# A decoder layer on one core: three seven-product pairs in each double gate block, and other paces for the background multiply-adds

## The chip, the cores and the metric

The kernel runs on one core of one Trainium2 chip. The metric is the device time of one execution in microseconds (us), as the median of repeated runs. The profile shows one execution, taken by the hardware profiler.

## The reference, cut to what matters

One layer of a hybrid decoder for 256 tokens of width 2048, all in float32. `h` is the normalised input, modulated by vectors that come out of `silu(c) @ w_ada`; that product has six segments of 2048 columns, and the later ones (for the second norm and the gates) aren't needed until late in the layer.

```python
mod = jax.nn.silu(c) @ w_ada[l] + b_ada[l]
shift1, scale1, gate1, shift2, scale2, gate2 = jnp.split(mod[:, None, :], N_MOD, axis=-1)
h = rms_norm(x, norm1_gain[l]) * (1 + scale1) + shift1
x = x + gate1 * mixing_sublayer(h, w_in[l], ...)
h = rms_norm(x, norm2_gain[l]) * (1 + scale2) + shift2
x = x + gate2 * swiglu(h, w_ffn_in[l], w_ffn_out[l])
...
proj = h @ w_in              # in mixing_sublayer; the last 3 * 2048 columns are gate_cols
...
g = jax.nn.sigmoid(gate_cols.reshape(b, t, N_BRANCH, d))
y = (g[:, :, 0] * (o_sb @ w_br_sb) + g[:, :, 1] * (o_dil @ w_br_dil) + g[:, :, 2] * (o_gla @ w_br_gla))
return y @ w_out
```

The change is in how `gate_cols` is computed and in when the products with `w_ada` are done.

## The kernel before, in words

The two row tiles of 128 tokens stay on chip, and every weight matrix is streamed from HBM once, in raw blocks of 512 KB (two chunks of 128 rows by 512 columns) by the queue of the SP engine. TensorE takes its operands in a rounded format, so each float32 operand is kept as a high and a low part: ScalarE casts the raw block to the high part `whi` (L165, L236), VectorE subtracts it from the raw block to get `wlo` (L166, L222), and each product is three matmuls in `mm3`: high by high (L173), with the low part of the weights (L174), with the low part of the activations (L175). Their names in the profile give the result, then the weight and the stationary operand; `H` are the parts of h.

The stages are: the modulation for the first norm; the input projection in four groups of chunks (the last is `LAST`), with the three attention branches behind it; the gate stage; the y stage (`y_block`, branch outputs by gates); the output projection; the second norm; eleven FFN units and their output.

The gate stage is this: three single `gate_block`s for the first 512 columns of each branch, then three `gate_pair`s, each for two column blocks of one branch at once. A `gate_pair` calls `fast_products` over eight chunk pairs in the order of `GATE_PAIRS`. A tuple there is (chunk pair, fast). A plain pair makes 8 block products, 24 matmuls. A fast pair makes them with 7, 21 matmuls, in the way of Strassen and Winograd: it needs sums of the four blocks of h (`sums_of_h`, made once) and of the four weight blocks (`load_pair`, on VectorE, in tiles A0 and A1, which are then split too), and at the end of the block the shared partial results are merged (L313 to L316 and L272). Before, pairs 4 and 5 of each double block are fast.

Raw blocks land in a ring of four `raw` tiles and whatever `more_raws` adds; the high and low parts lie in rings of four `whi` and `wlo`, and whatever `more_rooms` adds: X1 and X2, A9 and A10. Before, the double blocks have 5, 6 and 5 raw tiles (T3 and X2 added) and 6, 5 and 5 rooms. `load` runs up to `LOOK` = 3 pairs ahead of the products.

The later segments of the modulation are a background generator. Each step, a *multiply-add*, loads 512 KB of w_ada (L517, into AR0, AR1, KC or KD) and does one 128x1024 operation on VectorE (`ada_mac`, L421, into T4, T5 and others). `tick` is called in the loops of products, and lets out multiply-adds at `state["rate"]`. A multiply-add is issued after the split that `state["split"]` holds. Before, the generator starts with the last group's first blocks, but at a rate of 0, and gets its first rate, `RATE_IN` = 0.8, some blocks later; in the double gate blocks the rate is `RATE_PAIRS` = 0.42.

A scheduler puts the instructions in order for each engine from the program's order, priorities (`prio`) and the tiles that come free; each engine then runs its list in order.

Of the kernel before, what the change touches and what calls it, by code (L numbers as in the profile page):

```python
# [29 lines left out]
N_DIL = 6  # L30
N_GLA = 4
SEG_SHIFT1, SEG_SCALE1, SEG_GATE1, SEG_SHIFT2, SEG_SCALE2, SEG_GATE2 = range(6)
RATE_IN, RATE_MID, RATE_GATES, RATE_PAIRS, RATE_Y, RATE_LAST = 0.8, 0.6, 0.65, 0.42, 0.5, 0.7

RATES_OP, RATES_FFN, RATE_OUT = (0.85, 0.5, 0.0), (0.75, 0.9, 0.7, 0.6), 0.5
GATE2_CUT = 12
# [13 lines left out]
OUT_B = ((0, 0), (1, 0)) + tuple(x for a, b in zip((8, 9, 10, 11, 12, 13, 6, 7), (2, 3, 4, 5, 14, 15, 16, 17)) for x in ((a, 1), (b, 0)))  # L50
PAIRS = ((0, 0), (1, 0), (5, 1), (2, 0), (6, 1), (7, 1), (3, 0), (4, 0))
PAIRS_4 = ((0, 0), (1, 0), (4, 1), (5, 1), (2, 0), (6, 1), (7, 1), (3, 0))
GATE_PAIRS = ((0, 0), (1, 0), (4, 1), (2, 0), (3, 0), (5, 1), (6, 0), (7, 0))
FOUR = (2, 3, 5, 6, 8)
RANK = 16
ROW_N1, ROW_N2, ROW_SBQ, ROW_SBK, ROW_DILQ, ROW_DILK, ROW_GB, ROW_GG = 16, 32, 48, 49, 50, 51, 52, 56
# [24 lines left out]
def trunk(ctx: ExitStack, tc: tile.TileContext, I, out):  # L81
# [16 lines left out]
    def S(tag, shape, dtype=F32):  # L98
        return slot.tile(shape, dtype, tag=tag, name=nm(tag))
# [27 lines left out]
    def tick(n):  # L127
        state["due"] = state.get("due", 0.0) + n
        while state["due"] >= 1.0:
            state["due"] -= 1.0  # L130
            for work in (bg, after):
                if work and next(work[0], "end") == "end":
                    work.pop(0)
# [67 lines left out]
    def sums_of(sf, h, a, b):  # L201

        (a0, b0), (a1, b1) = ((x[:, a, :], x[:, b, :]) for x in h)
        for dst, x, y, op in (
            (0, a1, b1, ALU.add), (2, a0, a1, ALU.subtract), (1, sf[:, 0], a0, ALU.subtract), (3, b0, sf[:, 1], ALU.subtract)
        ):
            nc.vector.tensor_tensor(sf[:, dst], x, y, op=op)

    def load_pair(src, p, c0, c1, fast, tags):


        def raw_at(c):
            more_raws = state.get("more_raws", ())
            i = state["raws"] = (state.get("raws", -1) + 1) % (4 + len(more_raws))
            raw = S(more_raws[i], [P, 2, NB]) if i < len(more_raws) else wp.tile([P, 2, NB], F32, tag="raw", name=nm("raw"))
            nc.sync.dma_start(raw, src[2 * p * P : (2 * p + 2) * P, c : c + NB].rearrange("(k p) c -> p k c", p=P))
            return raw

        def sub(dst, x, y):
            chain = state.get("chain")  # L220
            with tc.issue_after(chain.ins) if chain is not None else nullcontext():
                done = nc.vector.tensor_tensor(dst, x, y, op=ALU.subtract)  # L222
            if "chain" in state:
                state["chain"] = done
            return done

        def split(src):
            n = src.shape[1]
            more_rooms = state.get("more_rooms", ())
            i = state["tiles"] = (state.get("tiles", -1) + 1) % (4 + len(more_rooms))  # L230
            if i < len(more_rooms):
                hi, lo = (S(tag, [P, 2, NB], F32R) for tag in more_rooms[i])
            else:
                hi = wp.tile([P, 2, NB], F32R, tag="whi", name=nm("whi"), bufs=4)
                lo = wp.tile([P, 2, NB], F32R, tag="wlo", name=nm("wlo"), bufs=4)
            nc.scalar.copy(hi[:, :n, :], src)  # L236
            state["split"] = sub(lo[:, :n, :], src, hi[:, :n, :].bitcast(F32))
            return [(hi[:, i, :], lo[:, i, :]) for i in range(n)]

        with prio():  # L240
            if not fast:
                return [split(raw_at(c0)), split(raw_at(c1))]
            r0, r1 = raw_at(c0), raw_at(c1)
            b11, b21 = split(r0)
            ta, tb = (S(tag, [P, 2, NB]) for tag in tags)
            sub(ta[:, 0], r1[:, 0], r0[:, 0])
            sub(ta[:, 1], r1[:, 1], r1[:, 0])
            (b22,) = split(r1[:, 1:2])
            sub(tb[:, 0], r1[:, 1], ta[:, 0])
            sub(tb[:, 1], r0[:, 1], tb[:, 0])  # L250
            t1, t3 = split(ta)
            t2, t4 = split(tb)
            return b11, b21, b22, t1, t3, t2, t4

    def fast_products(src, c0, c1, order, at, sums, own, other, tags, hooks={}, more=False, look=None):


        ws = []

        def load(n):  # L260
            while len(ws) < min(n, len(order)):
                ws.append(load_pair(src, order[len(ws)][0], c0, c1, order[len(ws)][1], tags))


        soon = AHEAD if hooks or more else 2 * AHEAD
        load(look or (LOOK if hooks else len(order)))
        o = [[own([P, NB]) for _ in range(NT)] for _ in range(2)]
        shared = []
        end = len(order)
        first_fast, last_fast = (f(n for n, (_, fast) in enumerate(order) if fast) for f in (min, max))  # L270
        last_plain = max(n for n in range(last_fast) if not order[n][1])
        add = lambda dst, x: nc.vector.tensor_tensor(dst, dst, x, op=ALU.add)  # L272

        def merge(half):
            with prio(soon):
                add(o[0][half], (first, third)[half])
                add(o[1][half], u[:, 1 - half])

        for n, (p, fast) in enumerate(order):
            tick(2 * state["rate"])  # L280
            if n in hooks:
                hooks[n]()
            load(n + LOOK)
            w = ws[n]
            if n == 1 and later:
                with tc.issue_after(state["mm"].ins), prio():
                    later.pop()()
            for half in range(2):
                if n == last_fast + 2 + half:
                    merge(half)  # L290
            merged = n > last_fast
            if fast:
                if not shared:
                    shared = [other([P, NB]) for _ in range(4)]
                    p1, p5, p7, p6 = shared
                s = sums[p]
                a, b = 2 * p, 2 * p + 1
                lefts = (at(a, 0), at(b, 0), s[3], s[0], s[2], s[1], at(b, 1))
                for dst, (h, l), (wh, wl) in zip((p1, o[0][0], o[1][0], p5, p7, p6, o[0][1]), lefts, w):
                    mm3(dst, h, l, wh, wl, n == first_fast and any(dst is x for x in shared), n == last_fast)  # L300
            else:
                for c in range(2):
                    for t in range(NT):
                        for k in range(2):
                            h, l = at(2 * p + k, t)

                            closed = n == end - 1 and not more or merged or (c, t) == (1, 1) and n == last_plain
                            mm3(o[c][t], h, l, *w[c][k], n == 0 and k == 0, k == 1 and closed, merged)
            if n == last_fast:
                with prio(soon):  # L310
                    u, first, third = S("KC", [P, 2, NB]), S("T6", [P, NB]), scr([P, NB])
                    nc.scalar.copy(first, p1)
                    nc.vector.tensor_tensor(u[:, 0], p6, first, op=ALU.add)  # L313
                    nc.vector.tensor_tensor(u[:, 1], p5, u[:, 0], op=ALU.add)
                    nc.vector.tensor_tensor(third, p7, u[:, 0], op=ALU.add)
                    nc.vector.tensor_tensor(u[:, 0], p5, third, op=ALU.add)  # L316
        for half in range(2):
            if end <= last_fast + 2 + half:
                merge(half)
        return o  # L320
# [822 lines left out]
        yield from last_macs()  # L1143

    bg.append(background())
    for b in range(0, 3):
        proj_block(LAST, b)
    qk_norm(sb_parts)
# [57 lines left out]
                gates[1 + i, br] = g  # L1206

    def sums_of_h():
        j = 2
        full = S("X1", [P, 4, T])  # L1210
        nc.vector.tensor_tensor(full, hT[0][j].bitcast(F32), hT[1][j].bitcast(F32), op=ALU.add)
        sf = S("X2", [P, 4, 2, P])
        sums_of(sf, [full[:, :, t * P : (t + 1) * P] for t in range(NT)], slice(0, 4, 2), slice(1, 4, 2))
        hi, lo = (S(tag, [P, 4, 2, P], F32R) for tag in ("T1", "T2"))
        nc.scalar.copy(hi, sf)
        nc.vector.tensor_tensor(lo, sf, hi.bitcast(F32), op=ALU.subtract)
        return {2 * j + m: [(hi[:, i, m, :], lo[:, i, m, :]) for i in range(4)] for m in range(2)}

    with prio():
        groups = dil_weights()  # L1220
# [91 lines left out]
    h_sums = sums_of_h()  # L1312
    state["rate"] = RATE_PAIRS
    ring["tags"], ring["spare"] = ("AR0", "AR1", "KD"), 1
    gate_pair(0, acc_bank, misc_bank, (("X1", "X2"), ("A9", "A10")), ("T3",))
    gate_pair(1, misc_bank, acc_bank, (("A9", "A10"),), ("X2", "T3"))
    gate_pair(2, acc_bank, misc_bank, (("A9", "A10"),), ("T3",))
    ring["tags"] = ("AR0", "AR1", "KC", "KD")
    ring["spare"] = 2
    state["rate"] = RATE_Y  # L1320
# [340 lines left out]
```

## Time and profile before

| | |
|---|---|
| median of 3 runs | 1577.7 us (1575.83 to 1578.93) |
| the profiled execution | 1579.31 us |
| its span, first to last instruction | 1577.5 us |
| mean granted TensorE clock | 0.999 |
| TensorE matmuls (PE) | 1564.6 us busy, 99% |
| VectorE (DVE) | 1394.3 us busy, 88% |
| ScalarE (ACT) | 876.0 us busy, 56% |
| DMA | 402.26 MB, mean 255 GB/s |

TensorE is busy nearly all the time. Busy shares of the other engines are averages over stages; the gate stage runs from about 492 to 622 us of the span, its double blocks are the part of it that the change edits, and the last group's first blocks lie around 250 us. A row of a timeline is: start in us, duration in us, engine, line, operation, out<-in, shape and count, and in brackets the idle time ahead of it with what ended it.

### The profile page before, as it was taken

What the parts mean: (1) busy time and instruction counts of PE and PEld (TensorE: products, weight loads), DVE (VectorE), ACT (ScalarE), POOL (GpSimd) and SP (SyncE); (2) the same over time, 40 slices, a digit from 0 to 9 for tenths busy, and PEclk for the clock granted to TensorE, in tenths of its full rate; (3) what the DMA queues carried; (4) which work ended last, traced back from release to release, by engine and by line L of the source; (5) the groups of instructions that cost most, each with busy time, mean ns of one, the idle gap of its engine ahead of it and who ended that gap; (6) DMA issues with size and microseconds to landing.
All of it is one profiled execution on the core that took longest, in us unless ns stands there. A gap on an engine that the chain in (4) does not pass through costs nothing.

```text
span 1577.5 us, 20267 instructions
## 1 busy us (share of the span) xinstructions
PE 1564.6 (99%) x7186; PEld 1294.6 (82%) x7186; DVE 1394.3 (88%) x1704; ACT 876.0 (56%) x1215; POOL 12.9 (1%) x24
## 2 busy tenths in 40 slices
PE   8999999999999999999999999999999999999998
PEld 7878888888888788888888888888888888888887
DVE  6889996888889899987977888999999999899896
ACT  5654448875765545344445645556555555455553
POOL 1000000000000000000000000000000000000000
PEclk9999999999999999999999999999999999999999
DMA  9999997677788888989897886565666566876664
GB/s 334 360 326 324 336 304 239 221 238 227 233 294 265 269 267 270 313 261 324 291 336 260 304 294 211 190 213 188 199 199 215 174 200 228 293 227 202 222 211 137
DMA packets 196317, 402.26 MB, mean 255 GB/s; under 512 B 13102, under 2 KB 28116, under 8 KB 196216
## 3 DMA queue, kind: packets, MB, share of 16 engines
q1 hardware_dynamic: 194952, 397.75, 75.8%
q0 software_dynamic: 1088, 3.16, 0.6%
q8 instruction: 56, 0.92, 0.2%
q14 instruction: 45, 0.37, 0.1%
q10 hardware_dynamic: 176, 0.07, 0.0%
HBM read 395.68 MB, written 5.24 MB: 254 GB/s over the span
## 4 chain that ended last, share of the span: by engine, by line
PE 89%; ACT 3%; DVE 3%; DMA 2%; issue 1%; POOL 0%; SPq 0%; DVEq 0%; ACTq 0%; POOLq 0%
PE acc L175 21%; PE acc L173 20%; PE acc L174 20%; PE misc L174 7%; PE misc L175 7%; PE misc L173 7%; DMA raw<-w_in 2%; ACT whi L165 1%; PE acc L576 1%; PE misc L945 1%; ACT scr L771 1%; PE misc L1284 1%; DVE wlo L166 1%; DVE A L222 1%; DVE wlo L222 0%
## 5 line engine op out<-in xcount | busy, mean ns | idle before, releaser
L165 ACT CAST whi<-raw 128x1024 fp32r<-128x1024 f32 (+1 forms) x277 | 278.7, 1012 | 286.4 <-PE acc L175 198.5
L166 DVE TENSOR_TENSOR wlo<-raw,whi 128x1024 fp32r<-128x1024 f32 (+1 forms) x277 | 322.0, 1171 | 93.2 <-ACT whi L165 92.0
L173 PE MATMUL acc<-whi,H 128*128 128x512 f32 x997 | 390.5, 392 | 0.9 <-ACT H L588 0.8
L174 PE MATMUL acc<-wlo,H 128*128 128x512 f32 x997 | 388.8, 390 | 0.8 <-DVE wlo L166 0.8
L175 PE MATMUL acc<-whi,H 128*128 128x512 f32 x997 | 388.8, 391 | 0.5 <-DVE H L595 0.4
L175 PEld LDWEIGHTS acc<-whi,H 128*128 128x128 f32 x997 | 187.0, 188 | 40.3 <-DVE H L595 1.4
L173 PEld LDWEIGHTS acc<-whi,H 128*128 128x128 f32 x997 | 187.2, 188 | 39.4 <-ACT H L588 1.3
L174 PEld LDWEIGHTS acc<-wlo,H 128*128 128x128 f32 x997 | 187.4, 188 | 39.1 <-DVE wlo L166 1.7
L236 ACT CAST whi<-raw 128x1024 fp32r<-128x1024 f32 (+1 forms) x130 | 125.3, 976 | 70.2 <-PE acc L175 32.4
L222 DVE TENSOR_TENSOR wlo<-raw,whi 128x1024 fp32r<-128x1024 f32 (+1 forms) x130 | 144.0, 1126 | 15.5 <-ACT whi L236 14.5
L175 PE MATMUL acc<-whi,A 128*128 128x512 f32 x221 | 86.1, 389 | 0.0
L173 PE MATMUL acc<-whi,A 128*128 128x512 f32 x210 | 82.0, 391 | 0.0
L174 PE MATMUL acc<-wlo,A 128*128 128x512 f32 x210 | 81.7, 389 | 0.0
L174 PE MATMUL misc<-wlo,H 128*128 128x512 f32 (+1 forms) x190 | 74.3, 391 | 2.0 <-DVE wlo L222 2.0
L173 PE MATMUL misc<-whi,H 128*128 128x512 f32 (+1 forms) x190 | 74.3, 391 | 0.0
L175 PE MATMUL misc<-whi,H 128*128 128x512 f32 (+1 forms) x190 | 74.0, 390 | 0.0
L222 DVE TENSOR_TENSOR A<-raw,A 128x1024 fp32r<-128x1024 f32 (+2 forms) x54 | 53.9, 1003 | 1.3 <-ACT A L236 1.0
L421 DVE SCALAR_TENSOR_TENSOR ada<-AR,csil,ada 128x1024 f32<-128x1024 f32 x39 | 49.5, 1279 | 5.7 <-DMA AR<-w_ada 5.7
L175 PEld LDWEIGHTS acc<-whi,A 128*128 128x128 f32 x221 | 41.5, 188 | 8.7
L236 ACT CAST A<-raw 128x1024 fp32r<-128x1024 f32 (+1 forms) x36 | 35.9, 1002 | 21.8 <-PE acc L175 8.9
L174 PEld LDWEIGHTS acc<-wlo,A 128*128 128x128 f32 x210 | 39.4, 188 | 8.1
L173 PEld LDWEIGHTS acc<-whi,A 128*128 128x128 f32 x210 | 39.4, 188 | 8.0
(682 smaller groups left out, 3040.3 us busy)
## 6 DMA issues: line engine op xcount, KB each, us to landing
raw<-w_in SPq DMA_DIRECT2D x192, 512.0 KB, 4.9
raw<-w_ffn_in SPq DMA_DIRECT2D x135, 512.0 KB, 4.6
raw<-w_ffn_out SPq DMA_DIRECT2D x73, 512.0 KB, 5.1
AR<-w_ada SPq DMA_DIRECT2D x62, 512.0 KB, 4.8
raw<-w_out SPq DMA_DIRECT2D x32, 512.0 KB, 5.7
OS<-w_ada SPq DMA_DIRECT2D x24, 512.0 KB, 6.5
KD<-w_ada SPq DMA_DIRECT2D x22, 512.0 KB, 5.3
AR<-w_ffn_in SPq DMA_DIRECT2D x22, 512.0 KB, 4.1
```

The source lines that it names most:

```text
L165: state["cast"] = nc.scalar.copy(hi[:, :n, :], raw[:, :n, :])
L166: state["split"] = nc.vector.tensor_tensor(lo[:, :n, :], raw[:, :n, :], hi[:, :n, :].bitcast(F32), op=ALU.subtract)
L173: nc.tensor.matmul(ps, lh, rh, start=start, stop=False, skip_group_check=seeded)
L174: nc.tensor.matmul(ps, lh, rl, start=False, stop=False, skip_group_check=seeded)
L175: state["mm"] = nc.tensor.matmul(ps, ll, rh, start=False, stop=stop, skip_group_check=seeded)
L222: done = nc.vector.tensor_tensor(dst, x, y, op=ALU.subtract)
L236: nc.scalar.copy(hi[:, :n, :], src)
L421: nc.vector.scalar_tensor_tensor(acc, raw, c, acc, op0=ALU.mult, op1=ALU.add)
L576: state["warm"] = nc.tensor.matmul(ps, ones_r, wide, start=True, stop=True)
L771: nc.scalar.activation(junk, heads(b)[:, t, h, :], AF.Square, accum_out=ss[:, t, i : i + 1])
L945: nc.tensor.matmul(ps[:n, t * N_GLA + h, :].rearrange("p (s l) -> p s l", l=L), at(f, h, t)[:, :n], odd(at(f, h, t)), start=True, stop=True,)
L1284: nc.tensor.transpose(ps[:, i, :], src[:, i * P : (i + 1) * P], ident)
```

## The change

1. `GATE_PAIRS`: pairs 4, 5 and 6 of each double block are fast (before 4 and 5), and the order is plain 0, plain 1, fast 4, plain 2, fast 5, fast 6, plain 3, plain 7.
2. `sums_of_h` also makes the sums of h for pair 6. They lie in tile T3.
3. T3 is therefore no raw tile any more: the double blocks have 4, 5 and 4 raw tiles. The rooms stay.
4. In `fast_products` with `look` set, a multiply-add is issued after the split of the next pair, where before it was the latest pair loaded, which lies up to two pairs further on.
5. `RATE_PAIRS` goes from 0.42 to 0.25, and the background runs at `RATE_FIRST` = 0.3 from the last group's first block on.

```diff
-RATE_IN, RATE_MID, RATE_GATES, RATE_PAIRS, RATE_Y, RATE_LAST = 0.8, 0.6, 0.65, 0.42, 0.5, 0.7
+RATE_FIRST, RATE_IN, RATE_MID, RATE_GATES, RATE_PAIRS, RATE_Y, RATE_LAST = 0.3, 0.8, 0.6, 0.65, 0.25, 0.5, 0.7
...
-GATE_PAIRS = ((0, 0), (1, 0), (4, 1), (2, 0), (3, 0), (5, 1), (6, 0), (7, 0))
+GATE_PAIRS = ((0, 0), (1, 0), (4, 1), (2, 0), (5, 1), (6, 1), (3, 0), (7, 0))
...
-        ws = []
+        ws, splits = [], []
         def load(n):
             while len(ws) < min(n, len(order)):
                 ws.append(load_pair(src, order[len(ws)][0], c0, c1, order[len(ws)][1], tags))
+                splits.append(state["split"])
...
         for n, (p, fast) in enumerate(order):
+            if look:
+                state["split"] = splits[min(n + 1, end - 1)]
             tick(2 * state["rate"])
...
     bg.append(background())
+    state["rate"] = RATE_FIRST
     for b in range(0, 3):
         proj_block(LAST, b)
...
     def sums_of_h():
...
+        for p0, n, tags in ((4, 2, ("T1", "T2")), (6, 1, ("T3",))):
...
-    gate_pair(0, acc_bank, misc_bank, (("X1", "X2"), ("A9", "A10")), ("T3",))
-    gate_pair(1, misc_bank, acc_bank, (("A9", "A10"),), ("X2", "T3"))
-    gate_pair(2, acc_bank, misc_bank, (("A9", "A10"),), ("T3",))
+    gate_pair(0, acc_bank, misc_bank, (("X1", "X2"), ("A9", "A10")))
+    gate_pair(1, misc_bank, acc_bank, (("A9", "A10"),), ("X2",))
+    gate_pair(2, acc_bank, misc_bank, (("A9", "A10"),))
```

VectorE in the first double block, before, from the splits of its second and last fast pair (pair 5, whose raw tiles are T3 and raw_1062) to the splits of the two plain pairs behind it; L421 is a multiply-add:

```order
L222 TENSOR_TENSOR wlo_1068_4813<-raw_1062_4802,whi_1067_4812 128x512
L222 TENSOR_TENSOR A1_1066_4809<-raw_1062_4802,A0_1065_4808 128x512
L222 TENSOR_TENSOR wlo_1070_4819<-A0_1065_4808,whi_1069_4818 128x1024
L222 TENSOR_TENSOR A1_1066_4809<-T3_1061_4800,A1_1066_4809 128x512
L421 SCALAR_TENSOR_TENSOR T5_914_4128<-AR0_1000_4558,csil_91,T5_914_4128 128x1024
L222 TENSOR_TENSOR wlo_1072_4823<-A1_1066_4809,whi_1071_4822 128x1024
L421 SCALAR_TENSOR_TENSOR T5_914_4128<-AR1_1043_4722,csil_91,T5_914_4128 128x1024
L222 TENSOR_TENSOR X2_1076_4856<-raw_1074_4853,X1_1075_4855 128x1024
L421 SCALAR_TENSOR_TENSOR T4_913_4127<-AR0_1042_4695,csil_91,T4_913_4127 128x1024
L222 TENSOR_TENSOR A10_1079_4862<-raw_1077_4859,A9_1078_4861 128x1024
L222 TENSOR_TENSOR wlo_1083_4895<-raw_1081_4892,whi_1082_4894 128x1024
L222 TENSOR_TENSOR wlo_1086_4901<-T3_1084_4898,whi_1085_4900 128x1024
```

VectorE at the corresponding place after the change, from the first split of pair 6, the third fast one (raw tiles raw_1073 and raw_1074; L424 is now the multiply-add; wlo_1088 and wlo_1091 belong to plain pair 3, A10_1084 to pair 6):

```order
L222 TENSOR_TENSOR wlo_1076_4838<-raw_1073_4833,whi_1075_4837 128x1024
L222 TENSOR_TENSOR A0_1077_4841<-raw_1074_4835,raw_1073_4833 128x512
L222 TENSOR_TENSOR A0_1077_4841<-raw_1074_4835 128x512
L222 TENSOR_TENSOR wlo_1080_4846<-raw_1074_4835,whi_1079_4845 128x512
L222 TENSOR_TENSOR A1_1078_4842<-raw_1074_4835,A0_1077_4841 128x512
L222 TENSOR_TENSOR X2_1082_4852<-A0_1077_4841,X1_1081_4851 128x1024
L222 TENSOR_TENSOR A1_1078_4842<-raw_1073_4833,A1_1078_4842 128x512
L222 TENSOR_TENSOR wlo_1088_4889<-raw_1086_4886,whi_1087_4888 128x1024
L222 TENSOR_TENSOR wlo_1091_4895<-raw_1089_4892,whi_1090_4894 128x1024
L424 SCALAR_TENSOR_TENSOR T4_877_3929<-KD_1003_4543,csil_91,T4_877_3929 128x1024
L222 TENSOR_TENSOR A10_1084_4856<-A1_1078_4842,A9_1083_4855 128x1024
```

Before, the last split of a fast pair (wlo_1072) stands ahead of the splits of the next pair, with one multiply-add between; after, A10_1084, the last of pair 6, stands behind both splits of pair 3 and one multiply-add.

TensorE in the first double block, before, at the end of the products of pair 5:

```order
L173 MATMUL misc_1059_4775<-whi_1071_4822,T1_1012_4635 128x512
L174 MATMUL misc_1059_4775<-wlo_1072_4823,T1_1012_4635 128x512
L175 MATMUL misc_1059_4775<-whi_1071_4822,T2_1013_4636 128x512
L173 MATMUL acc_1039_4690<-whi_1071_4822,H2_17_114 128x512
L174 MATMUL acc_1039_4690<-wlo_1072_4823,H2_17_114 128x512
L175 MATMUL acc_1039_4690<-whi_1071_4822,H6_21_118 128x512
L173 MATMUL acc_1038_4689<-X1_1075_4855,H3_18_115 128x512
```

TensorE after the change, at the end of the products of pair 6 (A9_1083 and A10_1084 are high and low part of its last sums, whi_1087 and wlo_1088 those of pair 3):

```order
L173 MATMUL misc_1072_4811<-A9_1083_4855,T3_1020_4658 128x512
L173 MATMUL acc_1046_4712<-A9_1083_4855,H3_18_115 128x512
L173 MATMUL acc_1045_4711<-whi_1087_4888,H1_16_113 128x512
L174 MATMUL acc_1045_4711<-wlo_1088_4889,H1_16_113 128x512
L175 MATMUL acc_1045_4711<-whi_1087_4888,H5_20_117 128x512
L173 MATMUL acc_1045_4711<-whi_1087_4888,H1_16_113 128x512
L174 MATMUL acc_1045_4711<-wlo_1088_4889,H1_16_113 128x512
L174 MATMUL misc_1072_4811<-A10_1084_4856,T3_1020_4658 128x512
L175 MATMUL misc_1072_4811<-A9_1083_4855,T3_1020_4658 128x512
```

Before, the three matmuls of each product follow each other; after, two matmuls with A9_1083 and five of pair 3 stand ahead of the first one that reads A10_1084.

More of the change, by code (lines that the diff above doesn't have):

```diff
@@ L1208, in sums_of_h @@
     def sums_of_h():
[L1209 to L1217, printed above, removed]
+        out = {}
+        for p0, n, tags in ((4, 2, ("T1", "T2")), (6, 1, ("T3",))):
+            j, c = p0 // 2, slice(0, 2 * n)
+            full = S("X1", [P, 4, T])[:, c]
+            nc.vector.tensor_tensor(full, hT[0][j][:, c].bitcast(F32), hT[1][j][:, c].bitcast(F32), op=ALU.add)
+            sf = S("X2", [P, 4, 2, P])[:, :, :n]
+            sums_of(sf, [full[:, :, t * P : (t + 1) * P] for t in range(NT)], slice(0, 2 * n, 2), slice(1, 2 * n, 2))
+            if n == 2:
+                hi, lo = (S(tag, [P, 4, n, P], F32R) for tag in tags)
+            else:
+                hl = S(tags[0], [P, 2, 4, n, P], F32R)
+                hi, lo = hl[:, 0], hl[:, 1]
+            nc.scalar.copy(hi, sf)
+            nc.vector.tensor_tensor(lo, sf, hi.bitcast(F32), op=ALU.subtract)
+            for m in range(n):
+                out[p0 + m] = [(hi[:, i, m, :], lo[:, i, m, :]) for i in range(4)]
+        return out
     with prio():
```

## Prediction

> **What bounds the kernel now.** I read the page's busy times and its chain first, then the waits of TensorE, then the stretches of the gate stage, then the timeline around the one long wait.
>
> ```profile
> PE 1564.6 (99%) x7186; PEld 1294.6 (82%) x7186; DVE 1394.3 (88%) x1704; ACT 876.0 (56%) x1215; POOL 12.9 (1%) x24
> PE 89%; ACT 3%; DVE 3%; DMA 2%; issue 1%; POOL 0%; SPq 0%; DVEq 0%; ACTq 0%; POOLq 0%
> ```
>
> TensorE is the bound: 1564.6 of 1577.5 us. So time can leave in two ways only: fewer matmuls, or fewer and shorter waits in front of them. VectorE, at 88%, is the engine that can put waits there. The waits of TensorE over the whole span (sum, count, longest):
>
> ```profile
> PE misc L174 <- DVE wlo L222: 2.0, 1, 2.0
> ...
> PE acc L174 <- DVE wlo L166: 0.8, 2, 0.7
> ...
> PE misc L867 <- ACT A L792: 0.3, 1, 0.3
> ```
>
> Apart from start-up there is one long wait, for a low part that VectorE splits off (L222). It lies in the gate stage, which the change edits. The stage in stretches (busy us and starts of PE, PEld, DVE, ACT, POOL, then clock, DMA share, GB/s):
>
> ```profile
> 500.00:540.00 40.00, 40.00 (x178) 32.89 (x177) 37.38 (x43) 20.28 (x24) 0.00 (x0) 1.00 0.83 274
> 540.00:580.00 40.00, 38.03 (x161) 31.02 (x160) 35.40 (x39) 20.10 (x22) 0.00 (x0) 0.96 0.78 249
> 580.00:620.00 40.00, 40.00 (x178) 33.10 (x178) 37.48 (x41) 20.52 (x23) 0.00 (x0) 1.00 0.79 270
> ```
>
> An undisturbed stretch holds 178 matmuls in 40 us, 0.225 us each. The middle one holds 161: 17 fewer, so 17 x 0.225 = 3.8 us are lost there, and its clock is 0.96. The timeline of TensorE and, below it, of VectorE and the DMA queue shows how:
>
> ```profile
> 549.67 0.39 PE L173 MATMUL misc<-whi,H 128*128 128x512 f32 x1
> 552.03 0.50 PE L174 MATMUL misc<-wlo,H 128*128 128x512 f32 x1 [1.97 <-DVE wlo L222]
> ...
> 553.03 0.63 PE L174 MATMUL misc<-wlo,H 128*128 128x512 f32 x1
> 553.46 0.63 PE L175 MATMUL misc<-whi,H 128*128 128x512 f32 x1
> ...
> 556.01 0.40 PE L175 MATMUL misc<-whi,H 128*128 128x512 f32 x1
> ```
>
> ```profile
> 546.55 1.22 DVE L222 TENSOR_TENSOR wlo<-A,whi 128x1024 fp32r<-128x1024 f32 x1
> 547.68 1.28 DVE L421 SCALAR_TENSOR_TENSOR T<-KD,csil,T 128x1024 f32<-128x1024 f32 x1
> 550.15 0.69 DVE L222 TENSOR_TENSOR A<-X,raw 128x512 f32<-128x512 f32 x1 [1.18 <-DMA raw<-w_in]
> 550.76 1.22 DVE L222 TENSOR_TENSOR wlo<-T,whi 128x1024 fp32r<-128x1024 f32 x1
> ```
>
> ```profile
> 543.08 0.37 SPq L216 DMA_DIRECT2D raw<-w_in  x1
> ```
>
> A raw block of w_in that was issued at 543.08 is first read at 550.15, after 7.1 us. VectorE is in order, so a split that has its own data (550.76) stands behind it; TensorE waits 2.0 us for that split, and then runs about ten matmuls at a pitch of 0.43 us (553.03 to 553.46) until 556.01. The 3.8 us are 2.1 us of waiting and about 1.7 us of half clock.
>
> [...]
>
> **The change, part by part.**
>
> *Matmuls.* A seven-product pair issues 21 matmuls for a plain pair's 24. One pair more in each of three double blocks takes 3 x 3 = 9 away, which the changed order of instructions confirms (128x512 matmuls fall by nine): 9 x 0.225 = 2.0 us off the binding engine.
>
> *VectorE, the extra pair.* A plain pair costs two splits of 128x1024. From 546.55 to 547.68 one takes 1.13 us, so a pair takes 2.3. A seven-product pair has three of these and five of 128x512, which take 0.61 each (550.15 to 550.76): 3 x 1.13 + 5 x 0.61 = 6.4 us. The difference is 4.1 us a pair, 12.4 us in three blocks. The sums of h for one more chunk pair are one time only (four 128x128, one 128x512 and one split, about 2 us) and stand ahead of the stage, where the first products don't need them.
>
> *VectorE, the multiply-adds.* From the first split of chunk pair 2 in double block 0 to the first split of the y stage, the order of before has 18 multiply-adds and the order after has 12. They take about 1.2 us each:
>
> ```profile
> 541.18 1.28 DVE L421 SCALAR_TENSOR_TENSOR T<-AR,csil,T 128x1024 f32<-128x1024 f32 x1
> 542.37 0.68 DVE L222 TENSOR_TENSOR A<-raw,A 128x512 f32<-128x512 f32 x1
> ```
>
> So 6 x 1.2 = 7.2 us leave this stretch. Two of the six are then done already, since the background begins at the last column group's first block; four come later, the last of them where the FFN begins and all that is left is flushed. The stretch (first row), the last FFN unit, an FFN unit with multiply-adds, and the last group's first blocks:
>
> ```profile
> 502.06:616.69 114.63, 112.66 (x489) 92.57 (x489) 104.89 (x115) 56.75 (x64) 0.00 (x0) 0.99 0.81 269
> ```
>
> ```profile
> 1302.00:1344.00 42.00, 42.00 (x191) 34.88 (x190) 38.96 (x49) 23.75 (x28) 0.00 (x0) 1.00 0.69 241
> ```
>
> ```profile
> 922.00:965.00 43.00, 43.00 (x196) 35.67 (x195) 34.43 (x34) 20.70 (x23) 1.07 (x2) 1.00 0.84 279
> ...
> 1007.00:1049.00 42.00, 42.00 (x191) 34.86 (x190) 41.55 (x52) 25.15 (x30) 0.00 (x0) 1.00 0.61 201
> ```
>
> ```profile
> 246.00:282.00 36.00, 35.71 (x182) 29.59 (x181) 20.60 (x31) 30.87 (x77) 1.28 (x1) 1.00 0.75 236
> ```
>
> VectorE's work in the stretch becomes 104.9 + 12.4 - 7.2 = 110.1 us. TensorE, without its old loss and with nine matmuls fewer, would cross it in 114.6 - 3.8 - 2.0 = 108.8 us. So VectorE is 1.3 us over full use, and lives on its lead. The multiply-adds flushed where the FFN begins fall where VectorE is busy 34.4 of 43 us, and cost nothing; those moved to the first blocks fall where it is busy 20.6 of 36 us.
>
> *The lead.* How far VectorE is ahead of TensorE shows in when a split is made and when it is first used, at the two ends of the stretch:
>
> ```profile
> 502.06 1.21 DVE L222 TENSOR_TENSOR wlo<-raw,whi 128x1024 fp32r<-128x1024 f32 x1
> ```
>
> ```profile
> 507.34 0.39 PE L173 MATMUL acc<-whi,H 128*128 128x512 f32 x1
> ```
>
> That is 5.3 us at the first split of chunk pair 2.
>
> *New waits, S.* The two adjacent seven-product pairs are the place to look. Three small mixture operations take 1.3 us there:
>
> ```profile
> 499.69 1.26 DVE L1260 SCALAR_TENSOR_TENSOR A<-misc,vec,A 128x256 fp32r<-128x256 f32 x3
> ```
>
> In double block 0, from the first split of pair 2 through the last split of pair 6, the new order has on VectorE: pair 2 (2.3), pair 5 (6.4), pair 6 (6.4), both splits of pair 3 that are placed ahead of pair 6's last one (2.3), two multiply-adds (2.4) and three mixture operations (1.3): 21.1 us. TensorE first runs 24 + 21 + 16 matmuls and six that its order pulls ahead: 67 x 0.225 = 15.1 us, plus the lead of 5.3: 20.4. The split is late by 0.7 us. If VectorE also waits for the raw blocks of pair 5, which can be issued only when pair 4's are read out, 3.6 us of work before they are needed (three mixture operations and two splits, 1.3 + 2.3), some 1.5 us more are lost against a landing of 5.0:
>
> ```profile
> raw<-w_in SPq DMA_DIRECT2D x32, 512.0 KB, 5.0
> ```
>
> That makes 2.2 us. Blocks 1 and 2 have the same pattern. So S lies between 0 and 3 x 2.2 = 6.6 us. The low end is the last FFN unit (1302 to 1344): same order of plain and seven-product pairs, four raw buffers, TensorE busy all 42 us. And with VectorE busy 41.55 of 42 us in another unit, TensorE also shows no wait. I take 3 x 0.7 = 2.1 us, nearer to those units, since they are the same work. Waits as short as 0.8 and 0.3 us stand in the rows on TensorE's waits.
>
> *The old wait.* Its cause, a raw block that lands late ahead of a ready split, can come back anywhere; what it then costs is in S. The wait itself is tied to a buffer order that no longer exists (T3 and X2 as raw buffers in block 1), so I count its 3.8 us as gone.
>
> *Waiting one pair less far ahead.* A multiply-add that waits for the split of the next pair, and not of the latest one loaded, stands earlier in VectorE's queue. Its own w_ada block, if late, would then hold up the splits behind it; VectorE's waits of the gate stage bound that at 3.0 us in two waits, hidden under the lead unless it is used up:
>
> ```profile
> DVE wlo L222 <- ACT whi L236: 4.7, 7, 1.8
> ...
> DVE T L421 <- DMA AR<-w_ada: 3.0, 2, 1.7
> ...
> DVE A L222 <- DMA X<-w_in: 1.7, 1, 1.7
> DVE A L222 <- DMA raw<-w_in: 1.7, 2, 1.2
> ```
>
> *Sum.* -2.0 (matmuls) - 3.8 (old wait and its half clock) + 2.1 (new waits) = -3.7 us. The profiled execution took 1579.3 us, 1577.5 of span and 1.8 around it, and becomes 1575.6. It lies 1.6 us above the median of 1577.7, so the forecast for the median is 1574.0.
>
> **The rivals.** A measurement of this kernel can tell some 0.2%, 3.2 us, from no change.
>
> *The waits use up the gain: no change.* VectorE waits 1.5 us for raw blocks in each block, on top of the 0.7. S = 6.6, the sum is +0.8, the time 1578.5. For it: one raw buffer fewer in each block, and 9.7 us of waiting that VectorE has in the stretch already (114.6 - 104.9). Against it: the FFN units.
>
> *Slower: each new wait brings half clock.* If a wait reaches the 1.97 us of the old one, it costs 1.7 us more. Three waits of 2.2 us then cost 3 x 3.9 = 11.7 us; the sum is +5.9, the time 1583.6. The place is the last split of pair 6, behind pair 3's splits and a multiply-add. It decides from the point at which the lead at pair 2 falls below 5.5 us with the landings at 5.0: 2.0 us late. For it: VectorE 1.3 us over full use, so that lead isn't won back between blocks. Against it: the 0.3 us wait of the rows above falls into 246 to 282 us, and the clock stays at 1.00 there. [...]
>
> *The loss is elsewhere: the last group's first blocks.* From 246 to 282 us ScalarE is busy 30.9 of 36 us. About four w_ada blocks now stand in the one DMA queue there. At 236 GB/s for a share of 0.75, the full rate is 315 GB/s and a block of 512 KB takes 1.7 us; if raw blocks on the critical path stand behind all four, 6.7 us. The sum is +2.8, the time 1580.5. Against it: the share of 0.75 leaves room.
>
> That the change doesn't do what it says is not a case here: nine matmuls fewer stand in the order.
>
> **How the numbers follow.** Forecast case, S from 0 to 3.7, 1571.9 to 1575.6: 0.45, of which 0.38 is faster by over 0.2% (below 1574.5). Waits use up the gain, 1575.6 to 1581: 0.24, all but 0.02 the same. Half clock, 1581 to 1586: 0.21, slower. First blocks: 0.10, half the same and half slower. Faster 0.38; same 0.07 + 0.22 + 0.05 = 0.34; slower 0.02 + 0.21 + 0.05 = 0.28. The range goes from 1571.5 to 1583.6, which leaves out about half of the half-clock case and some hundredths elsewhere. The likeliest case's own range is 1571.9 to 1575.6.
>
> **What would show it.** Right: starts of the stage's 40 us stretches all near 178, clock 1.00, no wait of TensorE on L222's wlo or A over 1 us, VectorE above 95% busy in the stage. Wrong: several such waits (on A10 or wlo of the pairs after the second seven-product pair) summing to over 4 us, any pitch of 0.43 us after one of them, or new waits between 240 and 290 us.

## The result, and the profile after

The change makes the kernel slower: 1581.2 us in the median of 16 runs (1577.9 to 1584.3) against 1576.7 us of 16 runs of the kernel before (1575.5 to 1578.9). The ratio is 1.0028, with a 95% interval from 1.0021 to 1.0035. The forecast was 1574.0 us. With more runs the median of before moved from 1577.7 to 1576.7, so the profiled execution of before (1579.3) lay 2.6 us above its median; that of after (1580.6) lies 0.6 below its own. Times and ratios, here and below, are of fast executions; two of one later kernel, of 2247 and 4061 us, are left out.

The page of the kernel after, its busy times and the engines of its chain:

```profile
PE 1563.8 (99%) x7177; PEld 1292.6 (82%) x7177; DVE 1409.0 (89%) x1728; ACT 878.8 (56%) x1220; POOL 12.4 (1%) x24
PE 84%; DVE 7%; ACT 4%; DMA 3%; issue 2%; SPq 0%; ACTq 0%; DVEq 0%
```

TensorE has nine matmuls fewer, and DVE's part of the chain grew from 3 to 7%: more of the time hangs on VectorE. The waits of TensorE:

```profile
PE misc L173 <- DVE A L1272: 2.6, 1, 2.6
...
PE misc L846 <- ACT T L841: 0.9, 1, 0.9
...
PE misc L870 <- ACT A L795: 0.3, 1, 0.3
PE misc L174 <- DVE wlo L222: 0.3, 1, 0.3
```

The waits for `wlo` of L222 are down to 0.3 us, and the splits of the three-pair blocks hardly show at all. The long wait is for L1272, which is neither a split nor a multiply-add. The same stretches as before:

```profile
500.00:540.00 40.00, 37.39 (x157) 30.29 (x156) 36.48 (x46) 22.55 (x27) 0.00 (x0) 0.96 0.67 214
540.00:580.00 40.00, 39.82 (x174) 32.32 (x173) 40.00 (x46) 20.16 (x23) 0.00 (x0) 1.00 0.76 242
```

The short stretch is now the first, with 157 of 178 matmuls: 21 x 0.225 = 4.7 us, where before 3.8 us were lost in the second. TensorE's timeline, then VectorE's and one line of ScalarE's:

```profile
508.61 0.39 PE L173 MATMUL acc<-whi,H 128*128 128x512 f32 x1
511.61 0.49 PE L173 MATMUL misc<-whi,T 128*128 128x512 f32 x1 [2.61 <-DVE A L1272]
...
512.75 0.63 PE L174 MATMUL acc<-wlo,H 128*128 128x512 f32 x1
513.17 0.63 PE L175 MATMUL acc<-whi,H 128*128 128x512 f32 x1
...
515.31 0.41 PE L174 MATMUL acc<-wlo,H 128*128 128x512 f32 x1
```

```profile
500.79 1.26 DVE L1272 SCALAR_TENSOR_TENSOR A<-misc,vec,A 128x256 fp32r<-128x256 f32 x3
...
505.69 0.69 DVE L222 TENSOR_TENSOR A<-raw,raw 128x512 f32<-128x512 f32 x1 [1.28 <-DMA raw<-w_in]
...
509.78 1.29 DVE L222 TENSOR_TENSOR A<-raw,A 128x512 fp32r<-128x512 f32 x2
510.98 0.87 DVE L1272 SCALAR_TENSOR_TENSOR A<-misc,vec,A 128x256 fp32r<-128x256 f32 x2
```

```profile
511.89 0.47 ACT L1271 ACTIVATE A<-misc,vec 128x256 fp32r<-128x256 f32 x1 [5.55 <-DVE A L1272]
```

The kernel takes the outputs of its matmuls from PSUM, in banks named `acc` and `misc`; every matmul row here writes to one of the two. L1271 (ScalarE) and L1272 (VectorE) read the four misc banks that hold the transposed output of the third attention branch (`o_gla` of the reference, the GLA output). The first fast pair of double block 0 puts its shared results into misc banks, so the matmul at 511.61 has to wait until such a bank has been read. Before the change the last of these reads on VectorE was this one:

```profile
503.20 0.47 DVE L1260 SCALAR_TENSOR_TENSOR A<-misc,vec,A 128x256 fp32r<-128x256 f32 x1
```

Now the last three stand behind six operations of pair 5 and both splits of pair 2, and pair 5's first sum waits 1.28 us for a raw block. TensorE waits 2.6 us and then runs at a pitch of 0.42 to 0.43 us until 515.3; its granted clock is 0.50 from 512 to 515 us, and 1.00 from 516 on.

### The profile page after: what moved, and what is told of

Read it like the earlier page. It is cut to its first block, busy times and chain, and to the rows that moved or that the text cites. A ratio compares the mean times of both kernels' runs of the same rounds, so it can differ in the third digit from the quotient of the medians.

```text
span 1578.8 us, 20279 instructions
## 1 busy us (share of the span) xinstructions
PE 1563.8 (99%) x7177; PEld 1292.6 (82%) x7177; DVE 1409.0 (89%) x1728; ACT 878.8 (56%) x1220; POOL 12.4 (1%) x24
## 4 chain that ended last, share of the span: by engine, by line
PE 84%; DVE 7%; ACT 4%; DMA 3%; issue 2%; SPq 0%; ACTq 0%; DVEq 0%
PE acc L175 19%; PE acc L174 19%; PE acc L173 19%; PE misc L174 7%; PE misc L175 7%; PE misc L173 7%; DVE wlo L222 2%; DMA raw<-w_in 2%; ACT whi L165 1%; DVE A L222 1%; DVE wlo L166 1%; PE acc L579 1%; PE misc L948 1%; ACT scr L774 1%; DVE KD L222 1%
## 5 line engine op out<-in xcount | busy, mean ns | idle before, releaser
L165 ACT CAST whi<-raw 128x1024 fp32r<-128x1024 f32 (+1 forms) x277 | 278.7, 1011 | 284.2 <-PE acc L175 154.0
L166 DVE TENSOR_TENSOR wlo<-raw,whi 128x1024 fp32r<-128x1024 f32 (+1 forms) x277 | 322.3, 1173 | 90.4 <-ACT whi L165 88.8
L174 PE MATMUL acc<-wlo,H 128*128 128x512 f32 x1006 | 392.9, 391 | 0.8 <-DVE wlo L166 0.8
L175 PEld LDWEIGHTS acc<-whi,H 128*128 128x128 f32 x1006 | 188.9, 188 | 40.7 <-DVE H L598 1.4
L173 PEld LDWEIGHTS acc<-whi,H 128*128 128x128 f32 x1006 | 189.1, 188 | 40.4 <-ACT H L591 1.3
L236 ACT CAST whi<-raw 128x1024 fp32r<-128x1024 f32 (+1 forms) x142 | 137.6, 976 | 83.1 <-PE acc L175 43.9
L222 DVE TENSOR_TENSOR wlo<-raw,whi 128x1024 fp32r<-128x1024 f32 (+1 forms) x142 | 157.9, 1126 | 13.9 <-ACT whi L236 12.8
L174 PE MATMUL misc<-wlo,H 128*128 128x512 f32 (+1 forms) x204 | 79.1, 388 | 0.1
L175 PE MATMUL misc<-whi,H 128*128 128x512 f32 (+1 forms) x204 | 79.0, 387 | 0.0
L173 PE MATMUL misc<-whi,H 128*128 128x512 f32 (+1 forms) x204 | 78.6, 389 | 0.0
L222 DVE TENSOR_TENSOR A<-raw,A 128x512 f32<-128x512 f32 (+2 forms) x63 | 57.1, 914 | 0.6 <-ACT A L236 0.2
L424 DVE SCALAR_TENSOR_TENSOR ada<-AR,csil,ada 128x1024 f32<-128x1024 f32 x40 | 51.0, 1278 | 7.3 <-DMA AR<-w_ada 7.3
L236 ACT CAST whi<-A 128x1024 fp32r<-128x1024 f32 x28 | 29.4, 1054 | 32.9 <-DVE A L222 25.9
```

The source lines that it names most:

```text
L165: state["cast"] = nc.scalar.copy(hi[:, :n, :], raw[:, :n, :])
L166: state["split"] = nc.vector.tensor_tensor(lo[:, :n, :], raw[:, :n, :], hi[:, :n, :].bitcast(F32), op=ALU.subtract)
L173: nc.tensor.matmul(ps, lh, rh, start=start, stop=False, skip_group_check=seeded)
L174: nc.tensor.matmul(ps, lh, rl, start=False, stop=False, skip_group_check=seeded)
L175: state["mm"] = nc.tensor.matmul(ps, ll, rh, start=False, stop=stop, skip_group_check=seeded)
L424: nc.vector.scalar_tensor_tensor(acc, raw, c, acc, op0=ALU.mult, op1=ALU.add)
```

## The experiments

Theory A: the loss is this wait for banks. Theory B: VectorE has too little room in the double blocks, whatever stands first. Theory C: the earlier background costs, before 385 us. All medians below are of 9 to 16 runs but where said, and ratios are to the kernel before.

**Bank reads first.** The changed kernel with

```diff
-                nc.scalar.activation(dh, src, AF.Copy, scale=gcol)
-                nc.vector.scalar_tensor_tensor(dl, src, gcol, dh.bitcast(F32), op0=ALU.mult, op1=ALU.subtract)
+                with prio():
+                    nc.scalar.activation(dh, src, AF.Copy, scale=gcol)
+                    nc.vector.scalar_tensor_tensor(dl, src, gcol, dh.bitcast(F32), op0=ALU.mult, op1=ALU.subtract)
```

> The changed kernel, with ScalarE's and VectorE's reads of the four misc banks that hold the turned GLA output (8 pairs of operations) at raised priority, so that they stand on VectorE ahead of the sums of the first fast pair and not behind those of the second. Theory A (the loss is the bank wait): the changed kernel's trace has one wait of 2.6 us of TensorE for such a read at 508.6, with half clock behind it, 21 matmul starts or 4.7 us short in 500 to 540. That wait goes, the stretch holds 176 to 178 matmuls, and the time falls by 3.5 to 5 us against the changed kernel, to about 1576.5, a ratio to the kernel before of 1.000. Theory B (VectorE has too little room in the double blocks, whatever stands first): the 3 us of reads only move the lateness to the splits of pair 4 to 6; the sum of TensorE's waits in 492 to 622 stays above 2.5 us and the ratio above 1.002.

Measured: 1576.4 us, 1.0000 (0.9991 to 1.0009): 4.8 us less than the changed kernel. The wait is gone, and the stretches from 492 to 580 us are full:

```profile
492.00:540.00 48.00, 48.00 (x212) 39.45 (x211) 47.81 (x60) 28.77 (x36) 0.00 (x0) 1.00 0.75 250
540.00:580.00 40.00, 40.00 (x178) 33.11 (x177) 39.72 (x46) 22.96 (x27) 0.00 (x0) 1.00 0.79 257
```

VectorE is busy 87.5 of 88 us there and TensorE waits for nothing; from 580 to 622 us it still loses 0.7. Theory A holds for this wait; B does not, for this place.

**The kernel before once more.**

> The kernel before once more, for a second profiled execution. If its wait of 2.0 us near 550 with the half clock behind it (17 matmuls short) belongs to the kernel, it is there again, and the time of this execution is near 1579. If it belongs to single executions (a raw block that took 7.1 us to land), the new profile lacks it or has it elsewhere, its clock is 1.000 and its time is near the median of 1576.7. Then the 3.8 us that the prediction counted as gone were never in the median.

Measured: 1576.8 us, 0.9999 (0.9990 to 1.0007), span 1574.6. Its wait near 550 us is there again, but shorter, and without half clock:

```profile
550.53 0.50 PE L174 MATMUL misc<-wlo,H 128*128 128x512 f32 x1 [1.31 <-DVE wlo L222]
550.87 0.40 PE L175 MATMUL misc<-whi,H 128*128 128x512 f32 x1
```

```profile
540.00:580.00 40.00, 38.53 (x169) 31.28 (x168) 37.66 (x41) 21.41 (x25) 0.00 (x0) 1.00 0.83 272
```

So neither expectation is quite right: the wait is in both executions, its half clock in one of them. By the busy time 1.5 us are lost here, not 3.8.

**The changed kernel once more** (one execution).

> The changed kernel once more, for a second profiled execution, since the kernel before's two executions differed by 2.9 us in their spans. If the wait for the banks in double block 0 belongs to the kernel, it is there again near 508 us, of 1.5 to 2.6 us, and the stretch from 492 to 540 us holds 204 matmuls or fewer, where the kernel with the bank reads first holds 212. If it was one execution's, the stretch holds 211 or more.

Measured: 1580.4 us, span 1578.6. The wait for the banks is there at 510.5, with 1.5 us and no half clock. The number of matmuls (213) is no measure here, since small transposes in this stretch count as much as large matmuls; the busy time is, 46.45 of 48 us. This execution loses more before 385 us instead, here after and then the second execution of before:

```profile
PE misc L846 <- ACT T L841: 1.7, 2, 1.1
PE misc L173 <- DVE A L1272: 1.5, 1, 1.5
PE misc L870 <- ACT A L795: 1.2, 1, 1.2
```

```profile
246.00:385.00 139.00, 135.81 (x720) 113.24 (x719) 115.28 (x154) 101.24 (x194) 2.06 (x2) 1.00 0.71 228
```

```profile
246.00:385.00 139.00, 138.71 (x736) 116.08 (x736) 114.06 (x152) 103.38 (x200) 2.13 (x3) 1.00 0.69 223
```

The two losses don't simply add. TensorE reaches the bank 1.9 us later than in the first execution (its last matmul ahead of the wait starts at 510.48, then at 508.61), and the read that frees the bank comes only 0.8 us later (511.79, then 510.98); so what was lost earlier shortens the wait, by the 1.1 us that it is shorter. The granted clocks of the single runs tell how common the half clock is: of the 16 runs of the changed kernel six show 0.998, as the first profile does, with a mean of 1581.9 us, and four 1.000, as the second does, with 1580.1 us. Of the 11 runs with the bank reads first none is below 0.999.

**The third pairs alone**, with the rates, the look ahead and the start of the background as before:

```diff
-            if look:
-                state["split"] = splits[min(n + 1, end - 1)]
...
-    state["rate"] = RATE_FIRST
```

> The third fast pair, its sums and the smaller raw rings alone: RATE_PAIRS 0.42, multiply-adds behind the latest split, background from block 5 as before. Theory A: the bank reads stand at the same places among the splits, so the wait of about 2.6 us with its half clock comes again; 1.002 to 1.004 of the kernel before. Theory B: with more multiply-adds in the double blocks VectorE is further over its room, and the time is 4 us or more above the changed kernel: 1.005 or more.

Measured in 5 runs: 1583.0 us, 1.0037 (1.0024 to 1.0049). The ratio is in A's range, but not by A's wait: the banks cost only 0.5 us. What costs most lies behind the double blocks: the y stage loses 4.2 us in several waits, most of them for VectorE and none over 1.6 us:

```profile
622.00:700.00 78.00, 73.81 (x332) 59.29 (x332) 70.88 (x80) 31.02 (x36) 0.00 (x0) 1.00 0.90 299
```

```profile
PE acc L174 <- DVE wlo L166: 2.5, 4, 1.3
PE misc L1128 <- DVE T L1123: 1.8, 2, 1.6
```

So with the old rate of multiply-adds the trace shows B's cause, a late VectorE, and not A's; but the loss comes behind the double blocks, and B's 1.005 was too much.

**The paces alone.**

> The paces alone: background from the last group's first block at 0.3, RATE_PAIRS 0.25, multiply-adds behind the next pair's split; two fast pairs and the raw rings as before. Theory A and B alike: no new bank wait, VectorE with 7 us less work in the double blocks: 0.998 to 1.000. Theory C (the loss comes from the earlier start of the background, where the changed kernel's trace has four matmuls fewer in 282 to 385 us, with a new wait of 0.9 us): 1.0005 to 1.002, with that wait in its trace.

Measured: 1578.4 us, 1.0012 (1.0003 to 1.0021). A and B alike expected 0.998 to 1.000, and neither names this loss. In the profiled execution, which took 1580.6 us and so lies 2.2 above the median, the place that loses most is that of C, a wait of 2.8 us that ends at 279 us, with half clock behind it (the stretch's clock is 0.96):

```profile
246.00:282.00 36.00, 33.20 (x157) 27.17 (x156) 23.54 (x32) 28.88 (x73) 1.04 (x1) 0.96 0.77 244
```

```profile
PE misc L870 <- ACT A L795: 2.8, 1, 2.8
```

**The paces, and bank reads first.**

> The paces of the change and the bank reads first, but two fast pairs and the raw rings as before. Against the kernel with the bank reads first and three fast pairs (1576.4 us) this gives the price of the third pairs alone. If they still cost VectorE's room: 1573 to 1575 us, 0.998 to 0.999 of the kernel before. If they save their nine matmuls, 2.0 us, once the banks come free in time: 1578 us, 1.001.

Measured: 1578.2 us, 1.0014 (1.0005 to 1.0023). With three fast pairs it is 1576.4. The third pairs save 1.8 us here, close to the 2.0 us of their nine matmuls, once the banks come free in time; the two intervals just overlap (1.0005 to 1.0023 and 0.9991 to 1.0009), so the saving is hardly clear of the noise.

**Bank reads first in the kernel before.**

> The kernel before, with the same raised priority for the bank reads. Theory A: before, the reads are done before TensorE needs the banks, so nothing is gained: 0.9995 to 1.0005, and the wait of 1.3 to 2.0 us near 550 stays. If the priority helps for another reason than the changed order: 0.997 to 0.999.

Measured: 1574.6 us, 0.9987 (0.9978 to 0.9996), the fastest of all. That was not expected from A. The wait near 550 us is gone:

```profile
540.00:580.00 40.00, 40.00 (x177) 32.79 (x176) 39.25 (x44) 21.99 (x25) 0.00 (x0) 1.00 0.84 275
```

```profile
PE misc L174 <- DVE wlo L222: 0.2, 1, 0.2
```

The order of VectorE shows why: the priority moves more than the bank reads. In double block 1 the split of T now stands ahead of the sum that waits for the late raw block, not behind it:

```profile
548.59 1.22 DVE L222 TENSOR_TENSOR wlo<-T,whi 128x1024 fp32r<-128x1024 f32 x1
550.50 0.69 DVE L222 TENSOR_TENSOR A<-X,raw 128x512 f32<-128x512 f32 x1 [0.69 <-DMA raw<-w_in]
```

This run is also a fairer base for the change. With the bank reads first, neither side has the bank wait or a long wait near 550 us, and the change still costs 1.8 us (1576.4 against 1574.6, with intervals that overlap a little), where nine matmuls fewer should save 2.0: the bank wait is not all that the forecast missed.

**Where the paces cost.** Five runs take the background's earlier start away or do it alone.

> The changed kernel without RATE_FIRST: the background gets its first rate at the last group's block 5, as before. Theory A (the loss is the bank wait in double block 0) expects that wait again and 1.002 to 1.004 of the kernel before, the changed kernel's 1.0028 within 0.1%. Theory C (the earlier background costs some 1 to 3 us between 246 and 385 us) expects 1.0005 to 1.002.

> The kernel with the bank reads first, and the background from block 5 as before. Theory C expects 0.998 to 0.999 of the kernel before (1573 to 1575 us) and no wait in 246 to 385 us over 0.5 us. If the earlier background costs nothing, or if four multiply-adds more in the gate and y stages cost as much: 0.9995 to 1.0005.

> The kernel before with the other two paces alone: RATE_PAIRS 0.25 and multiply-adds behind the next pair's split, no RATE_FIRST. Theory C: nothing lost before 385 us; with fewer multiply-adds in the double blocks the rest must be done later, and where all of the first gate has to be there (700 to 880 us) up to 4 us are lost, as the two kernels with three fast pairs and no early background lost them: 1.001 to 1.003. If there is room later: 0.9985 to 1.000.

Without RATE_FIRST the changed kernel takes 1580.3 us, 1.0023 (1.0013 to 1.0032), still with the bank wait (1.5 us); with bank reads first 1578.3, 1.0012 (1.0003 to 1.0021); the kernel before with the lower RATE_PAIRS and the shorter look ahead alone 1579.9, 1.0026 (1.0017 to 1.0035). C's gain did not come, though nothing is lost before 385 us. All three lose about 4 us later, where the whole first gate is needed at the residual and the multiply-adds left over are let out at once; here the last of the three, and then the second execution of before:

```profile
700.00:880.00 180.00, 175.78 (x798) 144.89 (x797) 144.58 (x163) 86.37 (x116) 4.09 (x6) 1.00 0.89 308
```

```profile
700.00:880.00 180.00, 179.84 (x823) 148.53 (x822) 146.19 (x166) 86.39 (x116) 4.08 (x6) 1.00 0.88 304
```

> The kernel before with the earlier background alone (RATE_FIRST 0.3 from the last group's first block; RATE_PAIRS 0.42 and the old look ahead). Theory C (w_ada blocks between the raw blocks in the DMA queue delay a cast on ScalarE, and TensorE waits for it at 277 and 306 us): 1.0005 to 1.002 of the kernel before, 1577.3 to 1579.7, with TensorE busy under 138.3 us in 246 to 385 (138.7 in the undisturbed execution). If the paces cost in the double blocks and not here: 0.9995 to 1.0005.

> The same with RATE_FIRST 0.45: four w_ada loads before the first raw block that ScalarE waits for where 0.3 has two, and one multiply-add more by 280 us. Theory C: worse than the run above by 0.5 to 3 us, 1.001 to 1.004. If the earlier background is not the cause: the same as the run above within 0.05%.

Measured: 1576.7 us, 1.0005 (0.9997 to 1.0014), and 1577.3 us, 1.0005 (0.9996 to 1.0014). Both profiles lose 1.4 us in this stretch against the second execution of before, first 0.3 and then 0.45:

```profile
246.00:385.00 139.00, 137.33 (x728) 114.52 (x728) 116.71 (x156) 102.00 (x197) 2.85 (x3) 1.00 0.73 236
```

```profile
246.00:385.00 139.00, 137.30 (x729) 114.45 (x727) 121.05 (x159) 102.09 (x197) 1.91 (x2) 1.00 0.75 247
```

The first of these two executions took 1580.9 us, 4.2 above its median, with another wait of 2.2 us and half clock between 622 and 700 us (the stretch's clock is 0.98, and TensorE is busy 75.83 of 78 us). Over all profiles the early loss goes with the early background: the seven without it hold 138.5 to 138.7 us of TensorE's work in this stretch, and of the ten with it nine hold 135.8 to 138.3. But more loads don't make the loss larger, and the time over all moves by less than the interval. In the second execution of the changed kernel its chain can be read, ScalarE first, then the DMA queue:

```profile
271.08 1.05 ACT L165 CAST whi<-raw 128x1024 fp32r<-128x1024 f32 x1 [2.58 <-DMA raw<-w_in]
```

```profile
253.96 0.34 SPq L520 DMA_DIRECT2D AR<-w_ada  x1
...
260.61 0.33 SPq L520 DMA_DIRECT2D AR<-w_ada  x1
```

In the second execution of before this cast starts at 269.04 after 0.65 us, with no w_ada load in the queue from 246 to 274. But the tenth profile, of the paces with bank reads first, has the same two loads at the same places, an early cast and a full stretch:

```profile
253.92 0.34 SPq L520 DMA_DIRECT2D AR<-w_ada  x1
...
260.57 0.33 SPq L520 DMA_DIRECT2D AR<-w_ada  x1
```

```profile
268.80 1.06 ACT L165 CAST whi<-raw 128x1024 fp32r<-128x1024 f32 x1 [0.48 <-DMA raw<-w_in]
```

```profile
246.00:385.00 139.00, 138.71 (x736) 116.02 (x735) 117.70 (x156) 103.24 (x200) 2.95 (x3) 1.00 0.74 238
```

So the two loads alone don't make the cast late.

**The look ahead, and the places of single multiply-adds** (all with bank reads first).

> The kernel with the bank reads first, with multiply-adds issued behind the latest loaded pair's split as before. If waiting for the next pair only is worth something by itself: 1.001 to 1.003 of the kernel before, with new waits of TensorE on multiply-adds' neighbours in the double blocks. If the look ahead is worth nothing: 0.9995 to 1.0005.

> Bank reads first, three fast pairs, multiply-adds behind the latest split, and RATE_FIRST 0.5 for the last group's first three blocks and 0 for the next two, so that the first two extra multiply-adds stand 6 to 7 instructions earlier on VectorE, ahead of the places at which TensorE waits for ScalarE at 277 and 306 us; the rest of the order is that of the kernel with the bank reads first and the old look ahead (1575.6 us). If these multiply-adds cause the two waits (0.5 and 0.9 us there): 0.998 to 0.9995 of the kernel before and stretches from 246 to 385 us as before the change. If not: 0.9996, and the waits stay.

> The kernel of the run above, with two fast pairs in double block 0 and three in blocks 1 and 2: three matmuls more (0.7 us), 4 us less for VectorE in block 0. If VectorE's room in block 0 still costs: below the run above by 0.5 to 2 us. If not: above it by 0.7 us.

Measured: 1575.6 us, 0.9996 (0.9987 to 1.0005); 1575.7, 0.9994 (0.9986 to 1.0003); 1578.3, 1.0012 (1.0004 to 1.0021). The look ahead by one pair is worth nothing that can be measured. Moving two multiply-adds away from the early waits changes nothing in the time; in the profile the wait of 0.5 us at 277 us is gone, and the one at L844 stays, with 1.1 us: they don't cause that one. What does stays open; no run took the loads in the queue away alone. The old pairs in block 0 cost 2.7 us, more than either reading of that run; with their order three waits of TensorE for L223 return, 1.5 us together, and the stretch from 540 to 580 us is short again (39.13 us busy).

## Why the prediction was wrong, point by point

- *Matmuls, -2.0 us*: right as far as the noise lets it be told. 1.8 us, three fast pairs against two with bank reads first and the new paces.
- *The old wait, -3.8 us gone*: wrong in size. One profiled execution was taken for the kernel, and it had the half clock that the second did not have. The wait is worth 1.5 us in the second, and the run with bank reads first in the kernel before, in which it is gone, gains 1.9. The forecast's own hint, an execution 1.6 us above its median, was used only as an offset.
- *VectorE's work, 110.1 us in the stretch*: right in the sum, with some luck. The trace has 11 multiply-adds in the stretch where the prediction counted 12, and two more reads of the misc banks fall into it than before. The same stretch after, from its first split to the first split of the y stage, has 109.85 us:

```profile
503.19:619.04 115.85, 112.80 (x486) 91.67 (x485) 109.85 (x128) 62.69 (x72) 0.00 (x0) 0.99 0.72 230
```

- *New waits, S = 2.1 us at the last split of pair 6*: this is the step that failed. No wait came there. The wait came earlier, at the misc banks of the first fast pair, in one block and not three; it cost 4.7 us in the first execution and 1.5 in the second, and moving the reads to the front gained 4.8 us in the medians, together with what else the priority moves. The prediction even counted the operations in question, as "mixture operations" of 1.3 us; it took them for work in the queue, and didn't ask who waits for the bank that they read. They are the GLA output's reads.
- *The lead of 5.3 us* was carried over from before. After the change the first split of pair 2 starts at 503.19 and is first used at 506.57: 3.4 us.
- *Half clock after a wait of about 2 us* (the slower rival): right for this wait (2.61 us, and then a granted clock of 0.50 for 3.4 us), wrong in place and number. One such wait, not three; 4.7 us and not 11.7. That 1581.2 falls into this rival's band (1581 to 1586) is therefore luck. Apart from the wait at the start of the span (2.54 us before; the granted clock reads 1.00 from 0 to 8 us there, though the first three 128x512 matmuls take 1.65 us), those of 1.97, 2.2 (the earlier background alone, between 622 and 700 us), 2.61 and 2.80 us brought half clock, and those of 1.31, 1.54 and 1.6 us (the last with the third pairs alone, between 622 and 700 us, where the clock is 1.00) did not.
- *Multiply-adds moved at no cost*: wrong. The paces alone cost 1.7 us, and 3.6 with bank reads first on both sides (1578.2 against 1574.6). The rival on the last group's first blocks named one place: 1.4 us are lost there in the profiles with the earlier background alone, against 4 us between 700 and 880 without it when the rate in the double blocks is lower. That rival's sum was off by 0.2: 6.7 us on -3.7 make +3.0, not +2.8.

The medians add up: 1576.7 + 1.7 (paces) - 1.8 (third pairs) + 4.8 (bank wait, with all that the priority moves) = 1581.4, measured 1581.2. This is little of a test: the terms share their runs, and the sum has to come out but for the 0.2 us between the paces with and without bank reads first. Each median ratio also has an interval of about 1.4 us to either side. The sum isn't free of the order in which the parts are taken: the third pairs with the old paces cost 6.3 us, and the priority gains 1.9 us in the kernel before and nothing that can be told (0.2) with the paces. Open stays why the early loss is nothing in one execution and 2.9 us in another; the same loads stood in the queue in both.

## What to carry to other kernels

Before costing more work on an engine that feeds TensorE, list every buffer that TensorE's next instructions need, PSUM banks among them, and find who reads the bank last and what now stands ahead of that read. Here some 3 us of short reads at the front of the queue, with what else moved along, took 4.8 us away. And take a second profiled execution before a stall of a few microseconds becomes a term of a sum: here the same wait was worth 3.8 us in one and 1.5 in the other.

## What was not expected of the hardware

In these traces, apart from the start of the span, TensorE ran at half clock behind its waits of 1.97, 2.2, 2.61 and 2.80 us, and not behind those of 1.31, 1.54 and 1.6 us. Behind the waits of 1.97 and 2.61 us the granted clock was 0.50 for 3.4 us each, and they cost 3.8 and 4.7 us with it; behind that of 2.80 us the slow pitch lasted 3.7 us, from 279.4 to 283.1. Two executions of the same program differed by 2.9 us in span (1577.5 and 1574.6), with the same instructions in the same order.
